# Layer norm's affine on the vector engine, a new order of routing and first expert, and a branch moved, in a two-layer decoder trunk

## The chip, the cores and the metric

The kernel runs on one core of a Trainium2 chip. The core has a matrix engine (TensorE, PE in the profile, with its weight loads PEld), a vector engine (VectorE, DVE), a scalar engine (ScalarE, ACT), a programmable engine (GpSimd, POOL), a queue engine that issues DMAs (SyncE, SP) and 16 DMA engines. Each engine works through its own queue in order. The metric is the device time of one execution in microseconds (us), less is better.

## The reference

Two layers work on 512 tokens of width 1024, in float32. Each layer has a mixer (five kinds of attention on one input projection, each gated, summed and sent through one output projection `w_out`) and a hierarchical mixture of experts. After each of the two comes a layer norm of `alpha * h + sublayer`:

```python
h = layer_norm(ALPHA * h + mixer(h), ln1_g, ln1_b)     # (x - mean) * rsqrt(var + eps) * g + b
glog = h @ w_rg + b_rg                                 # 4 groups: the best one
elog = h @ w_re[group] + b_re[group]                   # 4 experts in it: the best two, softmax weights
y = sum over 16 experts e of weight[:, e] * ((silu(a) * u) @ w_down[e]),  a, u = split(h @ w_up[e])
h = layer_norm(ALPHA * h + y, ln2_g, ln2_b)
```

`w_up[e]` is 1024x512 and `w_down[e]` 256x1024. The output is h after the second layer.

## The kernel before, in words

**Products.** Nearly all products are made of three TensorE matmuls: each operand is split into a high part rounded to fp32r (ScalarE, `hi`, line 97) and the rest (a subtraction on VectorE or, for chosen weights, on GpSimd, `lo`, line 112), and high x high, high x low and low x high are summed in PSUM. Split weights live in five buffers (three `wh`, two `eh`), which `hl_slot` hands out in turn; the raw weights come by DMA through SP into 28 slots of 512 KB (20 `rp`, 4 `rw`, 4 `re`).

**Output projection with routing** (`w_out`, `rows_done`). The 512 tokens are four row tiles of 128. The projection works on tiles 0 and 1 over all of K, and then on tiles 2 and 3; of each pair the last five K pieces are done tile by tile, so that a tile ends while the next is still being multiplied. What follows on a finished tile is a Python generator whose steps a counter (`tick`, one per group of three matmuls, the waits given by `gap`) places among the next tile's matmuls: add the residual (line 1044) and take statistics (1045); four transposes per half, copied out by ScalarE (1111); the 20 router logits; mean and rstd (`norm`, whose power is a GpSimd operation); the layer norm itself; `route` (line 1136 to 1162), a chain of some fifteen operations on 4 to 20 columns that marks the two chosen experts in `M` and sums them in `cb`; and `places`, which ranks the tokens of each expert by two small matmuls (1173) and turns ranks into row numbers (`own`, `sidx`). Two indirect DMAs of GpSimd then scatter the tile's normalised rows to `xd`, sorted by expert (1185).

The layer norm is written as one ScalarE operation `(x - mean) * rstd` over 1024 columns (1064), a multiplication by g and an addition of b, both on GpSimd (1066, 1067). For the last tile it is done in halves, one of them on VectorE.

**Expert 0** doesn't wait for the scatter. A column mask per tile (`slots_one`, 1316: which of 112 slots does this token fill) is multiplied with the normalised rows on TensorE (`own_rows`, 1328: 16 matmuls of 112 columns per tile, 64 in all), which yields expert 0's rows already transposed; `expert_x` splits them. In the kernel before, tile 0's masks and products come before the last tile's rank and the other three after it.

**The expert loop** (`experts`, `expert_step`). For each expert of 112 rows at most: four pieces of `w_up` (`expert_up`, 24 matmuls), `swiglu` (ScalarE tanh, two VectorE operations), two transposes, `expert_down` (12 matmuls), while the rows of the next but one are fetched from `xd` (1332), transposed and split (`next_x`). The weights of expert 1 are split while expert 0 is at work. The rest of the routing (softmax weights, gather indices) is `route_rest`. Experts 14 and 15 are not written back: `keep` multiplies their outputs by the weights of the rows and splits them (ScalarE and VectorE, 101 and 113), and the combination multiplies them on TensorE with transposed masks.

**The branch.** If more than 112 tokens chose one expert, `past_capacity` computes the rest. Each engine's queue reads the largest count into a register and compares (line 1482); with these inputs the body is skipped. Before, this stands behind the `keep` of expert 14's output, whose PSUM bank (`pt`) the body would use.

**Order.** The program is traced in the order of the Python code; a scheduler then puts each engine's instructions in order by a model of the times, earlier code first among those ready, and sets semaphores. `issue_after(i)` forces the instructions of a block that run on i's engine behind i in that engine's queue.

Of the kernel before, what the change touches and what calls it, by code (L numbers as in the profile page):

```python
# [15 lines left out]
ALU = mybir.AluOpType  # L16
AX = mybir.AxisListType

P = 128
# [51 lines left out]
class Trunk:  # L71
# [51 lines left out]
    def tr(self, out, in_, k=P):  # L123
        self.nc.tensor.transpose(out, in_, self.ident[:k, :k])  # L124
# [817 lines left out]
    def affine(self, out, x, gb):  # L942
        self.nc.vector.tensor_tensor(out, x, gb[0], ALU.mult)
        self.nc.gpsimd.tensor_tensor(out, out, gb[1], ALU.add)
# [91 lines left out]
    def rows_done(self, t, o, hr, gb, pool):  # L1036
# [12 lines left out]
        if t == NT - 1:  # L1049
# [13 lines left out]
        for n in ((slice(0, D),) if t < NT - 1 else self.halves):  # L1063
            self.normed = nc.scalar.activation(hr[:, n], hr[:, n], AF.Identity, bias=shift, scale=r)
            e = nc.vector if n.stop == 512 else nc.gpsimd
            e.tensor_tensor(hr[:, n], hr[:, n], gb[0][:, n], ALU.mult)
            e.tensor_tensor(self.h1[:, t, n], hr[:, n], gb[1][:, n], ALU.add)
        mb = self.route(t, lg)
        yield self.gap[2]
        if t == NT - 1:  # L1070
            self.xT = self.sb(self.base, [P, 2, 2, KT, CAP], "xh", F32R)
            self.yb = self.sb(self.base, [P, 4, D], "xl")
            with self.tc.issue_after(added.ins):
                self.own_rows(0, range(self.own0, self.nown))
        self.places(t, mb)
        if t == NT - 1:
# [27 lines left out]
    def logits_in(self, x, half, pool):  # L1104
# [6 lines left out]
        self.nc.scalar.copy(xT, ps.rearrange("p (k q) -> p k q", q=P))  # L1111
# [29 lines left out]
    def route(self, t, lg):  # L1141
# [17 lines left out]
        V.tensor_copy(self.ev[:, t], v[:, 0, 0:2])  # L1159
        mb = self.sb(rp, [P, 16], "mb", BF16)  # L1160
        V.tensor_tensor(mb, M[:, 0], M[:, 1], ALU.add)
        V.tensor_tensor(self.cb[:, t + 1, :], self.cb[:, t, :], mb, ALU.add)
        return mb

    def places(self, t, mb):
# [13 lines left out]
        V.scalar_tensor_tensor(self.own[:, t], mb, -65536.0, slot, ALU.mult, ALU.add)  # L1179
# [3 lines left out]
        self.routed = V.tensor_copy(self.sidx[:, t, :], si)  # L1183
        for c in range(2):
# [61 lines left out]
    def swiglu(self, ps, pool, tag, n=P):  # L1246
# [3 lines left out]
        nc.scalar.activation(t, ps[:n, :DE], AF.Tanh, scale=0.5)  # L1250
# [4 lines left out]
    def past_capacity(self, l):  # L1255

        nc, A = self.nc, self.A
        for t in range(NT):
# [7 lines left out]
            for e in range(NE):  # L1266
# [10 lines left out]
                y = [self.ps("pt"), self.ps("pt")]  # L1277
# [8 lines left out]
    def load_pieces(self, l, n):  # L1286

        nc, A = self.nc, self.A
        while len(self.pieces) < min(n, 6 * NE):
# [4 lines left out]
            if j < 4:  # L1294
                v = t.rearrange("p (k f) -> p k f", k=2)
                nc.sync.dma_start(v, A["w_up"][l, e, 256 * j : 256 * j + 256, :].rearrange("(k p) f -> p k f", p=P))
            else:
                v = t.rearrange("p (k f) -> p k f", k=1)
                nc.sync.dma_start(v, A["w_down"][l, e, P * (j - 4) : P * (j - 3), :].rearrange("(k p) f -> p k f", p=P))
# [6 lines left out]
    def expert_split(self, n):  # L1306

        if n not in self.hl:
            tag, pool = self.hl_slot()
            self.hl[n] = self.split_w(self.pieces[n], tag, "pool" if (n % 6 in self.pool_lo if n >= self.npre else n in self.pre_pool) else "dve", pool)  # L1310
# [7 lines left out]
    def own_rows(self, e, ts):  # L1318
# [3 lines left out]
        for t in ts:  # L1322
            one = self.one[:, t]
            self.slots_one(one, e, t)
# [12 lines left out]
    def expert_x(self, e):  # L1337

        xh, xl = self.xT[:, e % 2, 0], self.xT[:, e % 2, 1]
        for g in range(2):  # L1340
# [9 lines left out]
            self.lo(xl[:, 4 * g : 4 * g + 4, :], v, xh[:, 4 * g : 4 * g + 4, :])  # L1350

    def expert_up(self, l, e, j):
# [5 lines left out]
        h, lw = self.expert_split(6 * e + j)  # L1358
# [6 lines left out]

# [319 lines left out]
```

## Time and profile before

| what | before |
|---|---|
| time, median of 3 runs | 1724.15 us (1722.12 to 1728.31) |
| the profiled execution | 1725.9 us, its span 1723.8 us |
| mean granted clock of TensorE | 0.967 |
| busy: TensorE, VectorE, ScalarE, GpSimd | 1608.3, 1257.8, 893.2, 356.6 us |
| DMA | 273.60 MB, mean 159 GB/s |

In a profile each row of a timeline is an instruction or a run of like ones: start, duration, engine, line, tile written and tiles read, count, and in brackets how long the engine had nothing to do before it and what ended that. [...] A wait that an engine's queue makes without a data operation shows as the queue (DVEq, PEq). Layer 0's projection with routing runs from about 585 to 665 us, its expert loop to 830; layer 1's from about 1436 to 1515 and to 1681. Output of layer 1's combination ends the span.

### The profile page before, as it was taken

The page shows a single profiled execution, that of the slowest core. Times are in us where ns is not written, and L with a number is a line of the kernel's source. Part 1 is how long each engine was busy: PE and PEld are TensorE (multiplying, and loading weights), DVE is VectorE, ACT ScalarE, POOL GpSimd, SP SyncE. Part 2 cuts the span into 40 slices and gives each one's busy share as a digit, 9 for nine tenths or more (in the row PEclk, how much of TensorE's full clock was granted, in tenths as well). Part 3 has the DMA queues.
Part 4 walks back from the last instruction along what each step waited for, and adds up shares of the span by engine and source line. Part 5 has one row for each costly group of instructions (what it writes and reads, how often), then busy time and mean ns, then how long its engine had stood idle before and what let it go on. Part 6 is the DMA issues. An engine that isn't in the chain of part 4 may idle for free. (4 is left out here: it accounts for less than half of the span.)

```text
span 1723.8 us, 22844 instructions
## 1 busy us (share of the span) xinstructions
PE 1608.3 (93%) x7936; PEld 1272.9 (74%) x7936; DVE 1257.8 (73%) x2512; ACT 893.2 (52%) x1689; POOL 356.6 (21%) x261
## 2 busy tenths in 40 slices
PE   8999999999999988999699999999999999789994
PEld 7877877787778766666587787777877787666672
DVE  6776648755794679988688756588567757798876
ACT  5644446443463434888456434464344634368872
POOL 0000011111112254333510000110101123533345
PEclk9999999989999988999799999999999999899997
DMA  8232322444329547997542222222322285499953
GB/s 252 62 95 71 78 67 62 118 103 124 105 78 316 192 161 236 385 379 278 187 141 62 83 86 66 77 61 85 101 79 62 86 301 180 152 313 381 377 182 125
DMA packets 254561, 273.60 MB, mean 159 GB/s; under 512 B 38666, under 2 KB 191360, under 8 KB 254432
## 3 DMA queue, kind: packets, MB, share of 16 engines
q1 hardware_dynamic: 241032, 223.98, 40.6%
q0 software_dynamic: 13312, 47.98, 8.0%
q8 instruction: 67, 1.10, 0.3%
q14 instruction: 62, 0.51, 0.1%
q10 hardware_dynamic: 88, 0.03, 0.0%
HBM read 239.18 MB, written 32.77 MB: 158 GB/s over the span
## 5 line engine op out<-in xcount | busy, mean ns | idle before, releaser
L161 PE MATMUL f<-xh,wh 128*128 128x512 f32 (+2 forms) x1920 | 631.2, 397 | 2.1 <-DVE ot L587 1.1
L161 PEld LDWEIGHTS f<-xh,wh 128*128 128x128 f32 (+1 forms) x1920 | 355.6, 188 | 76.9 <-ACT xh L97 1.3
L161 PE MATMUL f<-xl,wh 128*128 128x512 f32 (+2 forms) x960 | 381.0, 397 | 0.0
L793 POOL TENSOR_TENSOR mg<-mg,gt 128x512 f32<-128x512 f32 x64 | 96.7, 1511 | 978.4 <-DVE gt L792 978.4
L112 DVE TENSOR_TENSOR wh<-rw,wh 128x1024 fp32r<-128x1024 f32 (+3 forms) x172 | 228.1, 1332 | 52.1 <-ACT wh L97 50.8
L161 PEld LDWEIGHTS f<-xl,wh 128*128 128x128 f32 (+1 forms) x960 | 180.8, 188 | 36.7 <-DVE xl L112 0.2
L97 ACT CAST wh<-rw 128x1024 fp32r<-128x1024 f32 (+3 forms) x178 | 178.6, 1012 | 47.2 <-PE f L187 13.9
L783 ACT ACTIVATE gt<-f,bgh 128x512 f32<-128x512 f32 x80 | 55.1, 688 | 209.6 <-PE f L161 209.6
L116 PE MATMUL f<-wh,xh 128*112 128x512 f32 (+1 forms) x564 | 154.7, 402 | 3.1 <-DVE wh L112 2.1
L116 PE MATMUL f<-oh,bh 128*128 128x512 f32 x480 | 131.2, 400 | 0.1
L116 PEld LDWEIGHTS f<-wh,xh 128*112 128x112 f32 (+1 forms) x564 | 98.3, 179 | 33.8 <-DVE wh L112 3.3
L97 ACT CAST pth<-pt 128x128 fp32r<-128x128 f32 (+1 forms) x192 | 77.5, 418 | 87.2 <-PE pt L124 81.4
L792 DVE SCALAR_TENSOR_TENSOR gt<-gt,f 128x512 f32<-128x512 f32 x64 | 43.8, 685 | 105.6 <-PE f L116 101.1
L116 PE MATMUL f<-eh,xh 128*112 128x512 f32 (+1 forms) x396 | 112.0, 409 | 9.0 <-DVE eh L112 9.0
L112 DVE TENSOR_TENSOR ptl<-pt,pth 128x128 fp32r<-128x128 f32 (+1 forms) x192 | 88.9, 474 | 24.7 <-ACT pth L97 20.6
L97 ACT CAST wh<-rp 128x1024 fp32r<-128x1024 f32 x84 | 87.4, 1054 | 34.0 <-PE pt L116 20.7
L116 PE MATMUL s<-qk,qk 128*128 128x256 f32 (+7 forms) x416 | 98.3, 334 | 5.7 <-DVE st L249 2.6
L116 PEld LDWEIGHTS f<-oh,bh 128*128 128x128 f32 x480 | 88.9, 190 | 19.8 <-issue 1.0
L112 DVE TENSOR_TENSOR wh<-rp,wh 128x1024 fp32r<-128x1024 f32 x70 | 95.0, 1366 | 10.9 <-ACT wh L97 10.0
L116 PEld LDWEIGHTS f<-eh,xh 128*112 128x112 f32 (+1 forms) x396 | 69.9, 182 | 29.8 <-DVE eh L112 10.3
L124 PE MATMUL pt<-ident,ne 128*128 128x128 f32 x472 | 83.7, 279 | 8.5 <-DVE ne L428 3.8
L116 PEld LDWEIGHTS s<-qk,qk 128*128 128x128 f32 (+1 forms) x416 | 66.9, 192 | 26.5 <-DVE st L249 9.3
(366 smaller groups left out, 2851.4 us busy)
## 6 DMA issues: line engine op xcount, KB each, us to landing
rp<-in_w_up_dram SPq DMA_DIRECT2D x96, 512.0 KB, 14.1
rw<-in_w_gate_dram SPq DMA_DIRECT2D x80, 512.0 KB, 3.8
rp<-in_w_down_dram SPq DMA_DIRECT2D x48, 512.0 KB, 13.1
rw<-in_w_in_dram SPq DMA_DIRECT2D x38, 512.0 KB, 3.7
rw<-in_w_out_dram SPq DMA_DIRECT2D x32, 512.0 KB, 4.2
yd<-xl POOLq DMA_DIRECT2D x28, 448.0 KB, 7.0
xl<-xd POOLq DMA_DIRECT2D x24, 448.0 KB
rb<-in_w_br_dram SPq DMA_DIRECT2D x80, 128.0 KB, 3.0
```

Source lines behind the costliest of these rows:

```text
L97: return nc.scalar.copy(out, in_)
L112: return e.tensor_tensor(out, in_, hi.bitcast(F32), ALU.subtract)
L116: self.nc.tensor.matmul(out, lhsT, rhs, start=start, stop=stop)
L124: self.nc.tensor.transpose(out, in_, self.ident[:k, :k])
L161: self.nc.tensor.matmul(o[:M, n], a[:, k, :M], b[:, k, n], start=c + k + m == 0, stop=k == KT - 1 and m == 2, skip_group_check=cut > 1)
L783: nc.scalar.activation(t, gp, AF.Tanh, bias=self.bgh[:, b * 8 + f : b * 8 + f + 1], scale=0.5)
L792: nc.vector.scalar_tensor_tensor(t, t, 1.0, bp, ALU.add, ALU.mult)
L793: i = nc.gpsimd.tensor_tensor(m, m, t, ALU.add)
```

## The change

1. *Affine.* `mean_rstd` replaces `norm` in `rows_done` and leaves out the product of mean and rstd. The layer norm of the mixer is two VectorE operations per half row: `(x - mean) * g`, then `* rstd + b`; ScalarE and GpSimd no longer take part. They stand behind `counted`, the running count at the end of `route`. Tile 2's second half, and its scatter, come only after tile 3's `counted`; tile 3's halves come in `places`, behind its `own` and the mask for expert 0 and ahead of the row numbers `sidx`.
2. *Routing and selection.* The copy of the two maxima (`ev`) moves behind the count. `places` of a tile comes 4 ticks after its route (before 12). The masks for tiles 0 and 1 are made in tile 2's step and their products stand behind tile 3's logits; tiles 2 and 3 follow tile 3's rank.
3. *First splits.* No split of the projection's weights is on GpSimd. The four high parts of expert 0's `w_up` come behind the last copy of the transposed rows, their low parts, all on VectorE, behind the split of expert 0's rows. `first_up` orders expert 0's 24 matmuls by kind: eight high x high, eight low rows x high weights, eight high rows x low weights.
4. *Other orders in expert 0.* Weight loads from piece 28 on are held in SP's queue behind the load of the rows of expert 3. Expert 1's first splits come behind expert 0's tanh (high) and gate (low), its transposes behind expert 0's. One low part on GpSimd comes behind the last scatter.
5. *Branch.* The branch stands ahead of the `keep` of expert 14; its body takes the `s` banks in place of `pt`.

```diff
-    def split_w(self, raw, tag="wh", eng="dve", pool=None):
+    def after(self, i):
+        return self.tc.issue_after(i.ins) if i else ExitStack()
+
+    def split_w(self, raw, tag="wh", eng="dve", pool=None, after=(None, None)):
...
-        self.hi(h, raw)
-        self.lo(l, raw, h, eng=eng)
+        with self.after(after[0]):
+            self.hi(h, raw)
+        with self.after(after[1]):
+            self.lo(l, raw, h, eng=eng)
...
-        if t == NT - 1:
+        last = t == NT - 1
+        if t == NT - 2:
...
-            with self.tc.issue_after(added.ins):
-                self.own_rows(0, range(self.own0))
+            for i in range(t):
+                self.slots_one(self.one[:, i], 0, i)
         for half in range(2):
             self.logits(lp, xT[half], half)
-        nmu, r, shift = self.norm(st)
+        if last:
+            self.own_rows(0, range(t - 1))
+        nmu, r = self.mean_rstd(st)
...
-        for n in ((slice(0, D),) if t < NT - 1 else self.halves):
-            self.normed = nc.scalar.activation(hr[:, n], hr[:, n], AF.Identity, bias=shift, scale=r)
-            e = nc.vector if n.stop == 512 else nc.gpsimd
-            e.tensor_tensor(hr[:, n], hr[:, n], gb[0][:, n], ALU.mult)
-            e.tensor_tensor(self.h1[:, t, n], hr[:, n], gb[1][:, n], ALU.add)
+        def affine(half):
+            c = slice(512 * half, 512 * half + 512)
+            nc.vector.scalar_tensor_tensor(hr[:, c], hr[:, c], nmu, gb[0][:, c], ALU.add, ALU.mult)
+            return nc.vector.scalar_tensor_tensor(self.h1[:, t, c], hr[:, c], r, gb[1][:, c], ALU.mult, ALU.add)
         mb = self.route(t, lg)
+        with self.tc.issue_after(self.counted.ins):
+            if last:
+                self.late()
+            else:
+                affine(0)
+                if t < NT - 2:
+                    affine(1)
+                self.late = lambda: (affine(1), self.scatter(t))
         yield self.gap[2]
...
-        self.places(t, mb)
-        if t == NT - 1:
+        self.places(t, mb, (lambda: self.slots_one(self.one[:, t], 0, t), lambda: affine(0), lambda: affine(1)) if last else ())
+        if t == NT - 2:
+            with self.tc.issue_after(self.routed.ins):
+                self.slots_one(self.one[:, t], 0, t)
+        if last:
             with self.tc.issue_after(self.rank.ins):
-                self.own_rows(0, range(self.nown, NT))
-            self.expert_x(0)
+                self.own_rows(0, [t - 1, t])
+            with self.tc.issue_after(self.routed.ins):
+                self.expert_x(0)
...
+        with self.tc.issue_after(owned.ins):
+            for f in between:
+                f()
...
-                y = [self.ps("pt"), self.ps("pt")]
+                y = [self.ps("s"), self.ps("s")]
...
+            with self.after(self.held):
+                if j < 4:
+                    nc.sync.dma_start(v, A["w_up"][l, e, 256 * j : 256 * j + 256, :].rearrange("(k p) f -> p k f", p=P))
...
+    def first_up(self, l):
+
+        up = self.up[0] = self.ps("f")
+        xh, xl = self.xT[:, 0, 0], self.xT[:, 0, 1]
+        w = [self.expert_split(j) for j in range(4)]
+        for x, i in ((xh, 0), (xl, 0), (xh, 1)):
+            for k in range(KT):
+                self.mm(up[:CAP], x[:, k, :], w[k // 2][i][:, k % 2, :], x is xh and i == 0 and k == 0, i == 1 and k == KT - 1)
...
-        h, lw = self.expert_split(6 * e + 4 + j)
+        h, lw = self.expert_split(6 * e + 4 + j, (None, self.xlo if e + j == 0 else self.scat[-1] if e == 0 else None))
...
-                self.next_x(1)
+                with self.tc.issue_after(turned.ins):
+                    self.next_x(1)
...
-                with self.tc.issue_after((self.routed, self.glu, self.hid[1])[self.upa[j]].ins):
-                    self.expert_up(l, 1, j)
+                self.expert_up(l, 1, j, (self.tanh, self.glu))
...
-        first = self.keep(y, 0, ((self.ap, "pth"), (self.ap, "ptl")))
...
         with self.tc.If(n > self.cap):
             self.past_capacity(l)
+        first = self.keep(y, 0, ((self.ap, "pth"), (self.ap, "ptl")))
...
-                with tc.issue_after(self.routed.ins), tc.issue_after(self.scat[-1].ins):
-                    for j in range(self.npre):
-                        with ExitStack() as st:
-                            if j >= self.nearly:
-                                st.enter_context(tc.issue_after(self.normed.ins))
-                            self.expert_split(j)
+                self.held = i
+                for j in range(self.npre):
+                    self.expert_split(j, (self.copied, self.xlo))
...
-    pre_pool = 3, 4
+    pre_pool = 4,
-    gap, order = (3, 1, 12), "0m1mm021v3v2vc3v"
+    gap, order = (3, 1, 4), "0m1mm021v3v2vc3v"
-    wo_pool = ((1, 1), (1, 3), (1, 5))
+    wo_pool = ()
```

## Rows read from the trace of the kernel before

**Rows 1.** The page's busy time, share of the span and instructions of each engine.

```profile
PE 1608.3 (93%) x7936; PEld 1272.9 (74%) x7936; DVE 1257.8 (73%) x2512; ACT 893.2 (52%) x1689; POOL 356.6 (21%) x261
```

**Rows 2.** Stretch table for PE: stretch, its length, busy us (count), PEclk granted, DMA share, GB/s.

```profile
608.60:622.30 13.70, 12.96 (x43) 0.51 0.49 183
...
622.30:643.40 21.10, 20.88 (x107) 1.00 0.50 183
...
647.00:663.20 16.20, 12.23 (x56) 0.50 0.38 133
...
1476.60:1482.70 6.10, 6.09 (x16) 0.51 0.95 333
```

**Rows 3.** PE's timeline: start us, us, engine, line, operation, [idle before <-releaser].

```profile
607.94 0.50 PE L116 MATMUL f<-eh,xh 128*128 128x512 f32 x1 [2.80 <-DVE eh L112]
...
642.99 0.40 PE L116 MATMUL pv<-wh,xl 128*128 128x512 f32 x1
...
657.37 0.17 PE L1173 MATMUL pt<-mb,trib 128*128 128x16 bf16 x1 [3.97 <-DVE mb L1161]
...
657.39 8.45 PE L1328 MATMUL f<-hr,mg 128*128 128x112 f32 x48
...
673.67 0.96 PE L124 MATMUL s<-ident,xl 112*128 112x112 f32 x8 [1.62 <-DMA xl<-xd]
...
1476.61 0.79 PE L116 MATMUL f<-eh,xh 128*128 128x512 f32 x1 [3.40 <-DVE eh L112]
```

**Rows 4.** DVE's timeline around the routing of layer 0.

```profile
602.70 1.74 DVE L1137 SCALAR_TENSOR_TENSOR gk<-lg,gm,vec 128x4 f32<-128x4 f32 x1
...
645.78 0.68 DVE L1044 SCALAR_TENSOR_TENSOR hr<-hr,pv 128x512 f32<-128x512 f32 x1
...
652.34 0.22 DVE L1137 SCALAR_TENSOR_TENSOR gk<-lg,gm,vec 128x4 f32<-128x4 f32 x1
...
653.14 0.73 DVE L1066 TENSOR_TENSOR hr<-hr,lnp 128x512 f32<-128x512 f32 x1
...
653.91 2.16 DVE L1067 TENSOR_TENSOR mg<-hr,lnp 128x512 f32<-128x512 f32 x1
...
657.14 0.17 DVE L1161 TENSOR_TENSOR mb<-M 128x16 bf16<-128x16 f32 x1
...
658.77 2.35 DVE L112 TENSOR_TENSOR wh<-rp,wh 128x1024 fp32r<-128x1024 f32 x2
```

**Rows 5.** POOL's timeline around the routing of layer 0.

```profile
602.02 2.40 POOL L1067 TENSOR_TENSOR mg<-hr,lnp 128x1024 f32<-128x1024 f32 x1
...
661.13 1.96 POOL L1185 DMA_INDIRECT xd<-mg,sidx  x1 [0.30 <-DVE wh L112]
...
663.12 2.37 POOL L112 TENSOR_TENSOR eh<-rp,eh 128x1024 fp32r<-128x1024 f32 x1
```

**Rows 6.** Timelines of DVE (layer 0) and PE (layer 1) at the expert loop's end.

```profile
828.97 1.41 DVE L113 SCALAR_TENSOR_TENSOR ptl<-pt,rw,pth 112x512 fp32r<-112x512 f32 x2 [2.25 <-ACT pth L101]
...
835.28 0.75 DVE L1496 SCALAR_TENSOR_TENSOR mg<-xl,wc,mg 128x512 f32<-128x512 f32 x1 [4.90 <-DVEq L1482]
...
1684.77 0.76 PE L116 MATMUL f<-ptl,oo 112*128 112x512 f32 x1 [3.79 <-PEq L1482]
```

**Rows 7.** Stretch table, all engines: projection with routing, expert loop, both of layer 0.

```profile
600.00:640.00 40.00, 36.24 (x157) 28.77 (x157) 30.79 (x70) 12.55 (x14) 25.65 (x14) 0.83 0.48 173
...
676.00:804.00 128.00, 119.09 (x576) 87.41 (x575) 114.01 (x135) 104.31 (x148) 42.41 (x35) 1.00 1.04 375
```

**Rows 8.** SP's timeline (DMA issues) around the routing of layer 0.

```profile
661.15 1.64 SPq L1296 DMA_DIRECT2D rp<-in_w_up_dram  x2
...
670.05 1.29 SPq L1332 DMA_DIRECT2D xl<-xd  x3
```

**Rows 9.** Line 1482, the branch, on DVE's queue: durations in ns, first and last start.

```profile
L1482 DVEq COMPARE_BRANCH  x2: 68/70/72, 830.2 to 1680.2; - x2
...
L1482 DVEq EVENT_SEMAPHORE  x2: 21/21/21, 834.9 to 1685.2; - x2
```

More of the change, by code (lines that the diff above doesn't have):

```diff
@@ L940, in norm, with mean_rstd @@
         return mv[:, 0:1], mv[:, 2:3], mv[:, 3:4]
-    def affine(self, out, x, gb):
-        self.nc.vector.tensor_tensor(out, x, gb[0], ALU.mult)
-        self.nc.gpsimd.tensor_tensor(out, out, gb[1], ALU.add)
+    def mean_rstd(self, st):
+        nc = self.nc
+        mv = self.sb(self.rp, [P, 4], "mv")
+        nc.vector.bn_aggr(mv[:, 0:2], st)
+        nc.vector.tensor_scalar(mv[:, 1:2], mv[:, 1:2], LN_EPS, None, ALU.add)
+        nc.gpsimd.tensor_tensor(mv[:, 2:3], mv[:, 1:2], self.mhalf[:, 0:1], ALU.pow)
+        nc.vector.tensor_scalar(mv[:, 3:4], mv[:, 0:1], -1.0, None, ALU.mult)
+        return mv[:, 3:4], mv[:, 2:3]
     def ln_params(self, which, l, pool, tag):
@@ L1110, in logits_in @@
             self.tr(ps[:, j * P : (j + 1) * P], x[:, k * P : (k + 1) * P])
-        self.nc.scalar.copy(xT, ps.rearrange("p (k q) -> p k q", q=P))
+        self.copied = self.nc.scalar.copy(xT, ps.rearrange("p (k q) -> p k q", q=P))
         return xT
@@ L1158, in route, with places @@
             V.tensor_scalar(M[:, c], z[:, 1], v[:, 1, c : c + 1], None, ALU.is_equal)
-        V.tensor_copy(self.ev[:, t], v[:, 0, 0:2])
         mb = self.sb(rp, [P, 16], "mb", BF16)
         V.tensor_tensor(mb, M[:, 0], M[:, 1], ALU.add)
-        V.tensor_tensor(self.cb[:, t + 1, :], self.cb[:, t, :], mb, ALU.add)
+        self.counted = V.tensor_tensor(self.cb[:, t + 1, :], self.cb[:, t, :], mb, ALU.add)
+        with self.tc.issue_after(self.counted.ins):
+            V.tensor_copy(self.ev[:, t], v[:, 0, 0:2])
         return mb
-    def places(self, t, mb):
+    def places(self, t, mb, between=()):
         nc, rp = self.nc, self.rp
@@ L1178, in places @@
         V.tensor_tensor(slot, slot, rank, ALU.add)
[L1179 removed]
+        owned = V.scalar_tensor_tensor(self.own[:, t], mb, -65536.0, slot, ALU.mult, ALU.add)
+        with self.tc.issue_after(owned.ins):
+            for f in between:
+                f()
         si = self.sb(rp, [P, 2], "si")
@@ L1183, in places, with scatter @@
         self.routed = V.tensor_copy(self.sidx[:, t, :], si)
+        if t != NT - 2:
+            self.scatter(t)
+    def scatter(self, t):
+        nc = self.nc
         for c in range(2):
@@ L1349, in expert_x, with expert_up @@
             self.hi(xh[:, 4 * g : 4 * g + 4, :], v)
-            self.lo(xl[:, 4 * g : 4 * g + 4, :], v, xh[:, 4 * g : 4 * g + 4, :])
-    def expert_up(self, l, e, j):
+            self.xlo = self.lo(xl[:, 4 * g : 4 * g + 4, :], v, xh[:, 4 * g : 4 * g + 4, :])
+    def expert_up(self, l, e, j, after=(None, None)):
         if j == 0:
@@ L1357, in expert_up @@
         self.load_pieces(l, 6 * e + j + 1)
-        h, lw = self.expert_split(6 * e + j)
+        h, lw = self.expert_split(6 * e + j, after)
         up = self.up[e][:CAP]
@@ L1379, in experts @@
         self.up = {}
-        for j in range(4):
-            self.expert_up(l, 0, j)
+        self.first_up(l)
         for e in range(NE - 1):
@@ L1566, in layer @@
             pre = self.bufs(pre)
-            self.nhi, self.slot, self.pieces = 0, 0, []
+            self.nhi, self.slot, self.pieces, self.held = 0, 0, [], None
             nrp, nre = self.BUFS["rp"], self.BUFS["re"]
@@ L1612 @@
     orders = ('aaaqaaaaqaaaaaaaaaaaaqqa', 'gggqqgaaaaggaaaaaaggaaaaqqggggggaqqqqagagaaa', 'qaagaaggagqqaggaaaqaggaqaaaaqggaqqaaaaggqggqqggqq', 'ggqgaaaaaaaaaaagqgaaaggqagggggggqqqqgaaaaga', 'ggaaaaaaaaaggggggggaaaaaaaaaaaaaaaagaaaaaaaaaagggagg')
-    nearly = 3
-    upa = 0, 1
-    own0, nown, x1 = 0, 1, 0
-    halves = slice(512, D), slice(0, 512)
+    x1 = 0
     class _Pool:
```

24 lines of the change are left out of this document (9 added, 15 removed).

## The prediction

> **What bounds the kernel now.** I read the busy table first [rows 1]: TensorE is busy for 93% of the span and VectorE for 73%, so the kernel is TensorE's except where TensorE stands still or runs slowly. The slices of the page show such places at the same points of both layers: the output projection with the routing, and the end of the expert loop. Next came the stretch table with the granted clock [rows 2]. [...] Then TensorE's timeline [rows 3]: 2.80 us of idle time at 607.94 until VectorE had a weight half ready (it has a twin of the same size in layer 1, and a third stall there of 3.40 us); 3.97 us at 657.37 until the last tile's routing had its mask; 1.62 us at 673.67 until expert 1's rows had arrived. The low clock begins each time after TensorE sat idle or nearly so.
>
> Why VectorE is late is told by its own rows beside GpSimd's [rows 4, 5]. L1137 works on four numbers per partition. It takes 0.22 us at 652.34 and 1.74 us at 602.70, where it ends at 604.44; GpSimd's half of the affine, begun at 602.02, ends at 604.42. L1067 on VectorE (2.16 us from 653.91 against 0.73 for L1066, same shape) shows the same: VectorE stands still until a GpSimd operation on SBUF data is done. I count thirteen such places between 600 and 672 us, 1 to 2.4 us each, about 20 us; all but one lie under operations that this change takes from GpSimd.
>
> **The change, part by part.** The sum is made on the profiled execution: 1725.9 us, 2.1 more than its span, 1.75 more than the median of the runs (1724.15).
>
> *Projection (A).* Removed per layer: from GpSimd two operations of 2.40 us for each of three tiles, two halves for the fourth, and four weight splits of about 2.4 us (such a one is the row at 663.12); from ScalarE the normalisation. Added on VectorE: four fused operations per tile. The nearest row is L1496 with two SBUF operands and the same shape, 0.75 us [rows 6], so 3.0 us per tile, 12 per layer; and the four splits (three here, one after) at 1.2 us each (two in 2.35 us at 658.77), 4.8. It loses the 2.9 us of the last tile's half and about 18 us of standing still. VectorE's own balance is thus some 4 us in favour, and it has 9 us idle in 600 to 640 to fill [rows 7]. What TensorE can win: 2.80 idle plus half of the 12.96 busy us at clock 0.51, 9.2 us in layer 0; 2.8 + 3.4 + half of 6.09 in layer 1, 9.2 as well. I don't take all: VectorE now carries three more splits and two tiles' affine in the same stretch, which leaves it some 90% full, and a split queued behind 3 us of affine makes TensorE wait again. Bounds: 9.2, and 1 where VectorE becomes the limit. I take 6 per layer, nearer to the upper end because short waits (1 us) leave the clock alone in the expert stage, which shows 1.00 throughout [rows 7]. A = 12.
>
> *Routing of the last tile and selection (B).* Before, the last projection matmul ends at 643.4 and the last rank product starts at 657.37, 14.0 us later. VectorE's first addition for the tile came only at 645.78, behind the routing of tile 2. From 652.34 to 657.14 the route takes 4.8 us, of which 653.14 to 656.07 is the affine (2.9). After: the addition at about 645.0 (tile 2's routing ends sooner, but half an affine is queued ahead), 0.7 for it, 0.7 for four transposes, 0.6 for their copy, 1.0 for eight logit matmuls at the full clock, 3.3 for a route without affine and without standing still: 651.3, so 6.1 us sooner. The selection products of tiles 0 and 1 (32 of 64 matmuls) fit into that wait, where 16 went before; that also keeps TensorE from idling. After the rank, 32 matmuls are left and not 48 in 8.45 us. But they wait for VectorE, on which there now stand, one behind the other, tile 2's second affine half (1.5), four place operations and one selection column (0.8), and tile 3's affine (3.0): 5.3 us after the rank, then eight matmuls of 0.18, so 6.7. The four low halves of the first weights now all come behind the split of the rows (1.5 us later), 4.8 us on VectorE, while the new order gives TensorE 16 matmuls that need none of them. The last matmul of the first product then ends some 13.1 us after the rank; 14.7 before. One GpSimd split falls on these VectorE operations: 0 to 2.4 us as in [rows 5], I take 1.2. The rest of the routing (about 4 us on VectorE, before under the selection products) now falls into the expert loop, where VectorE is busy 114.01 of 128 us [rows 7]: free to 4 us, I take 1.5. Together 6.1 + 0.4 - 1.5 = 5 per layer; bounds 9 (nothing given back) and 0. B = 10.
>
> [...]
>
> *Scatter and loads.* Tile 2's scatter moves behind route 3 and half an affine, and tile 3's indices come after 3 us of affine, so the scatters end about 9.5 us after the rank; before 5.7 (661.13 + 1.96) [rows 5]. The load of expert 1's rows was issued at 670.05, 7 us after that, with weight loads issued ahead of it on SP [rows 8]. Those are now held behind it; with the memory to itself I take 3.5 us for the scatter to land and 3 for the load: 16 after the rank, as before (16.3). TensorE reaches those rows after the first expert's transposes, 15 to 16 after the rank. So I cost this at 0, bounds -1.6 (the wait at 673.67 goes) and +4. Holding back four weight loads costs nothing while the loop draws on 28 pieces ahead.
>
> *Smaller edits.* The copy of the two maxima behind the count and one operation less in the mean: 0.2 each, in the terms above. Places after 4 ticks instead of 12: in A. Expert 1's splits behind the gate's operations: 0, bounds -1 and +1; one VectorE operation of 1.2 sets both.
>
> *Branch (C).* VectorE weights expert 14's output until 830.4, then branches; its next operation starts at 835.28 after 4.90 us [rows 6]. Its compare starts at 830.2 and 1680.2, the event behind it at 834.9 and 1685.2 [rows 9], 4.7 and 5.0 us. With the branch ahead, it begins when the last split is done, some 3 to 4 us sooner, and the weighting (1.41) comes behind. So VectorE gains 2 to 3 us at each layer's end. TensorE's 3.79 us at 1684.77 shrinks by less, as its own branch comes no sooner than its last matmul. I take 2 in layer 0, where ScalarE's branch is next, and 3 in layer 1, whose tail is one chain. Bounds 0 and 4 each. C = 5.
>
> Sum: 12 + 10 + 5 = 27; 1725.9 - 27 = 1698.9, 1697 against the median. I say 1698.
>
> **Rivals.**
> 1. *VectorE becomes the bound of the projection.* For it: some 90% full by the count above, one queue in a fixed order. Against: the stalls of 2 us each go. A falls to 2 per layer, B to 3: 4 + 6 + 5 = 15, so 1711 (this and the next times on the profiled execution).
> 2. *The branch gives nothing.* TensorE's own branch ends when it did, and the weighting only moves behind: C = 0, 1704. [...]
> 3. *The loop is paced by its loads.* DMA share 1.04 through the expert stage [rows 7]. Then B is lost and four held loads of 1.4 us (0.52 MB at 375 GB/s) cost 5.6 in each layer: 27 - 10 - 11 = 6, 1720. Against: no TensorE wait there is on a weight load.
> 4. *Slower: expert 1's rows come late.* The scatter goes behind 3 us of affine and another scatter, and TensorE's order puts the transposes ahead of matmuls that could run. If the rank comes no sooner (it must gain under 4 us for this to decide), the wait grows by 4 us, the clock drops, and some 10 busy us at half speed cost 5: 9 per layer, with A and B at nothing: +18 - 5, 1739.
>
> **How the numbers follow.** My forecast 0.58 (own range 1689 to 1706), rival 1 0.20, rival 2 0.08, rival 3 0.06, rival 4 0.08. The low end takes A and B at their upper bounds (-18 - 18) and C at 5: 1685, against the median 1683. The high end passes rival 1 and stops short of rival 3: 1717. A change under 0.3%, 5.2 us, can't be told from none. Rival 3 lies at that bound, most of it within; with the upper edge of rival 1 that makes 0.06 for the same, 0.08 for slower (rival 4), 0.86 for faster.
>
> **What would show it.** Right: no VectorE operation of 16 columns over 1 us before the rank product; TensorE's clock at 1.00 from 600 to 640 us; from the last projection matmul to the last rank under 10 us; 32 selection matmuls behind it; VectorE's wait for the branch ended before 832. Wrong: TensorE waits over 2 us for a weight half in the projection, or for expert 1's rows; splits stretched to 2.4 us with GpSimd idle; a branch that ends where it did.

## The result, and the profile after

The changed kernel takes 1698.31 us (median of 4 runs, 1694.69 to 1704.04) against 1725.2 before: ratio 0.9847, 95% interval 0.981 to 0.9885. In a second comparison it is 0.9846 (0.9826 to 0.9866). The profiled execution takes 1701.36 us, its span 1699.6, 24.2 less than before. The forecast was 1698; how it was reached held less well than the number.

The span can be cut at instructions that both kernels have, so that each stage has a length of its own. These rows are from TensorE's timeline of the kernel before; the other cuts stand in [rows 3]:

```profile
577.68 0.50 PE L116 MATMUL f<-wh,xh 128*128 128x512 f32 x1
...
758.65 0.38 PE L124 MATMUL pv<-ident,sw 112*128 112x112 f32 x2
...
822.62 0.35 PE L124 MATMUL pv<-ident,sw 112*128 112x112 f32 x2
...
838.91 0.64 PE L124 MATMUL pv<-ident,gt 112*128 112x112 f32 x2 [1.79 <-DVE mg L1496]
...
1427.86 0.73 PE L116 MATMUL f<-wh,xh 128*128 128x512 f32 x2
...
1494.20 0.40 PE L116 MATMUL pv<-wh,xl 128*128 128x512 f32 x1
...
1507.34 0.17 PE L1173 MATMUL pt<-mb,trib 128*128 128x16 bf16 x1 [3.68 <-DVE mb L1161]
...
1608.95 0.38 PE L124 MATMUL pv<-ident,sw 112*128 112x112 f32 x2
```

The same view of the changed kernel: first and last projection matmul, last rank product, the selection products behind it, three transposes that waited for a late gate in the expert loop, the transposes of the ninth expert (e = 8), those on both sides of the branch, and layer 1:

```profile
577.49 0.73 PE L116 MATMUL f<-wh,xh 128*128 128x512 f32 x2
...
632.51 0.40 PE L116 MATMUL pv<-wh,xl 128*128 128x512 f32 x1
...
641.65 0.17 PE L1198 MATMUL pt<-mb,trib 128*128 128x16 bf16 x1 [2.77 <-DVE mb L1184]
...
643.37 5.77 PE L1361 MATMUL f<-hr,mg 128*128 128x112 f32 x24 [0.57 <-DVE mg L1081]
...
672.78 0.41 PE L124 MATMUL pv<-ident,sw 112*128 112x112 f32 x2 [1.31 <-DVE sw L1286]
683.84 0.61 PE L124 MATMUL pv<-ident,sw 112*128 112x112 f32 x2 [2.05 <-DVE sw L1286]
696.40 0.39 PE L124 MATMUL pv<-ident,sw 112*128 112x112 f32 x2 [1.63 <-DVE rw L1272]
...
746.44 0.38 PE L124 MATMUL pv<-ident,sw 112*128 112x112 f32 x2
...
810.40 0.35 PE L124 MATMUL pv<-ident,sw 112*128 112x112 f32 x2
...
820.87 1.96 PE L124 MATMUL s<-ident,rw 128*128 128x128 f32 x8 [3.09 <-ACTq L1522]
824.53 0.61 PE L124 MATMUL pv<-ident,gt 112*128 112x112 f32 x2 [1.70 <-DVE gt L1286]
...
1413.92 0.95 PE L116 MATMUL f<-wh,xh 128*128 128x512 f32 x3
...
1469.00 0.40 PE L116 MATMUL pv<-wh,xl 128*128 128x512 f32 x1
...
1478.15 0.17 PE L1198 MATMUL pt<-mb,trib 128*128 128x16 bf16 x1 [2.78 <-DVE mb L1184]
...
1585.54 0.38 PE L124 MATMUL pv<-ident,sw 112*128 112x112 f32 x2
```

The differences of these starts (us), with those of the fifteenth and sixteenth experts' transposes, which bracket the branch:

| stage | layer 0, before to after | layer 1 | won in both |
|---|---|---|---|
| first to last projection matmul | 65.3 to 55.0 | 66.3 to 55.1 | 21.6 |
| to the last rank | 14.4 to 9.1 | 13.1 to 9.2 | 9.2 |
| to the ninth expert's transposes | 101.3 to 104.8 | 101.6 to 107.4 | -9.3 |
| to the fifteenth's | 64.0 to 64.0 | 64.0 to 64.0 | 0 |
| over the branch to the sixteenth's | 16.3 to 14.1 | 16.4 to 14.7 | 3.9 |
| all else (start, attention, tail) | | | -1.2 |

The sum is 24.2. Of the last row, -0.9 lies behind layer 1's branch, from the sixteenth expert's transposes to the end of the span (34.5 to 35.4 us). The projection won nearly twice what was forecast; what the routing won, the first experts gave back in full.

The stretch table (length, then busy us of PE, PEld, DVE, ACT, POOL; granted clock as a share of full speed; DMA share; GB/s) of the changed kernel shows both:

```profile
600.00:640.00 40.00, 38.88 (x225) 32.38 (x225) 34.92 (x118) 15.77 (x19) 7.83 (x7) 1.00 0.51 175
660.00:700.00 40.00, 35.02 (x166) 26.27 (x165) 38.04 (x67) 29.23 (x42) 11.68 (x10) 0.96 1.04 382
```

Against [rows 7], GpSimd's 25.65 us in 600 to 640 have become 7.83 and the clock 0.83 has become 1.00. VectorE does 34.92 of 40, and up to the last projection matmul (600 to 632.5) TensorE waits for none of it: it is busy for 32.50 of 32.50 us. In 660 to 700 VectorE is full (38.04 of 40). There POOL's and DVE's timelines show why two of the gates are late:

```profile
680.32 2.47 POOL L112 TENSOR_TENSOR wh<-rp,wh 128x1024 fp32r<-128x1024 f32 x1 [1.14 <-ACT wh L97]
...
692.71 2.43 POOL L112 TENSOR_TENSOR wh<-rw,wh 128x1024 fp32r<-128x1024 f32 x1 [1.22 <-issue]
```

```profile
680.47 2.35 DVE L1248 TENSOR_TENSOR rw<-rw 128x8 f32<-128x8 f32 x1
...
682.81 0.41 DVE L1285 SCALAR_TENSOR_TENSOR sw<-sw,f 112x256 f32<-112x256 f32 x1
...
692.88 2.28 DVE L1267 TENSOR_TENSOR rw<-rw 128x8 f32<-128x8 f32 x1
695.09 0.41 DVE L1285 SCALAR_TENSOR_TENSOR sw<-sw,f 112x256 f32<-112x256 f32 x1
```

L1248 and L1267 belong to `route_rest` and work on eight numbers per partition, for which the other operations of `route_rest` take 0.15 to 0.17 us in this stretch. They last until GpSimd's split ends (682.79, 695.14), and the gate (L1285) stands behind them: those are TensorE's waits of 2.05 and 1.63 us. Before, `route_rest` lay at 662 to 671 us, under the selection and expert 0's first product; two of its operations lasted 2.59 and 2.38 us there too, and no gate had to wait for them.

### The profile page after: what moved, and what is told of

Same layout as the page of the kernel before. It is cut to its first block, busy times and chain, and to the rows that moved or that the text cites. A ratio compares the mean times of both kernels' runs of the same rounds, so it can differ in the third digit from the quotient of the medians.

```text
span 1699.6 us, 22822 instructions
## 1 busy us (share of the span) xinstructions
PE 1596.7 (94%) x7936; PEld 1265.4 (74%) x7936; DVE 1244.5 (73%) x2540; ACT 882.9 (52%) x1679; POOL 299.8 (18%) x237
## 5 line engine op out<-in xcount | busy, mean ns | idle before, releaser
L112 DVE TENSOR_TENSOR wh<-rw,wh 128x1024 fp32r<-128x1024 f32 (+1 forms) x174 | 228.0, 1316 | 51.8 <-ACT wh L97 50.7
L97 ACT CAST wh<-rw 128x1024 fp32r<-128x1024 f32 (+3 forms) x178 | 178.5, 1012 | 49.6 <-PE f L192 14.1
L797 DVE SCALAR_TENSOR_TENSOR gt<-gt,f 128x512 f32<-128x512 f32 x64 | 43.7, 684 | 105.8 <-PE f L116 101.3
L124 PEld LDWEIGHTS pt<-ident,ne 128*128 128x128 f32 x472 | 54.8, 141 | 42.4 <-issue 17.1
## 6 DMA issues: line engine op xcount, KB each, us to landing
rp<-in_w_down_dram SPq DMA_DIRECT2D x48, 512.0 KB, 13.1
```

Source lines behind the costliest of these rows:

```text
L97: return nc.scalar.copy(out, in_)
L112: return e.tensor_tensor(out, in_, hi.bitcast(F32), ALU.subtract)
L124: return self.nc.tensor.transpose(out, in_, self.ident[:k, :k])
L797: nc.vector.scalar_tensor_tensor(t, t, 1.0, bp, ALU.add, ALU.mult)
```

## The experiments

All in one table, by the cuts above (layer 0 / layer 1). The last column is fifteenth to sixteenth expert, over the branch. The medians of the kernel before in the three comparisons were 1728.88 (affine_back, branch_back, rest_hid, rest_spread), 1727.7 (before_affine2, the two pool kernels, first_old) and 1726.76 us (the other four).

| kernel | time us (runs) | projection | to rank | to ninth expert | branch |
|---|---|---|---|---|---|
| changed, again (after_again) | 1702.06 (5) | 55.1 / 55.1 | 9.2 / 9.2 | 104.9 / 106.7 | 13.9 / 15.3 |
| affine_back | 1715.97 (4) | 63.2 / 61.4 | 11.3 / 11.2 | 104.3 / 104.9 | 14.0 / 14.6 |
| split_back | 1711.68 (1) | 63.9 / 60.7 | 7.9 / 7.9 | 106.3 / 106.3 | 13.9 / 13.4 |
| before_affine2 | 1716.25 (5) | 60.9 / 62.4 | 10.6 / 10.6 | 103.6 / 103.9 | 16.0 / 16.9 |
| pool_read | 1721.65 (1) | 56.0 / 56.0 | 9.9 / 9.9 | 115.4 / 115.0 | 14.0 / 13.9 |
| pool_write | 1701.07 (1) | 55.1 / 55.1 | 9.2 / 9.3 | 106.1 / 106.9 | 13.4 / 14.2 |
| branch_back | 1702.31 (4) | 55.0 / 55.0 | 9.1 / 9.1 | 103.3 / 107.4 | 15.5 / 17.0 |
| first_old | 1698.76 (1) | 55.1 / 55.1 | 9.2 / 9.2 | 103.8 / 103.8 | 14.2 / 15.2 |
| rest_hid | 1693.36 (4) | 55.1 / 55.1 | 9.2 / 9.2 | 105.9 / 105.6 | 13.8 / 13.9 |
| rest_spread | 1695.74 (4) | 55.1 / 55.0 | 9.1 / 9.1 | 104.1 / 105.4 | 13.9 / 14.8 |
| rest_fine | 1691.81 (5) | 55.1 / 55.0 | 9.2 / 9.2 | 103.4 / 102.3 | 13.8 / 13.8 |
| rest_fine_old | 1692.93 (5) | 55.1 / 55.1 | 9.2 / 9.2 | 103.3 / 102.1 | 13.9 / 14.7 |

The projection's length repeats within 0.1 us where nothing in it is changed; the loop's does not. The changed kernel's order gives 103.3 to 104.9 us in layer 0 (three profiles, branch_back among them) and 106.7 to 107.4 in layer 1.

**What made the projection faster.** Three kernels undo or do one part.

affine_back:

```diff
-        nmu, r = self.mean_rstd(st)
+        nmu, r, shift = self.norm(st)
...
-            nc.vector.scalar_tensor_tensor(hr[:, c], hr[:, c], nmu, gb[0][:, c], ALU.add, ALU.mult)
-            return nc.vector.scalar_tensor_tensor(self.h1[:, t, c], hr[:, c], r, gb[1][:, c], ALU.mult, ALU.add)
+            nc.scalar.activation(hr[:, c], hr[:, c], AF.Identity, bias=shift, scale=r)
+            nc.gpsimd.tensor_tensor(hr[:, c], hr[:, c], gb[0][:, c], ALU.mult)
+            return nc.gpsimd.tensor_tensor(self.h1[:, t, c], hr[:, c], gb[1][:, c], ALU.add)
```

> The changed kernel with the layer norm's affine put back on ScalarE (normalise) and GpSimd (two operations per half); the new order of routing, splits, selection and loads stays. Theory (the standing-still of VectorE under GpSimd operations is what cost the time in the projection): the projection slows to half clock again, last projection matmul some 8 to 11 us later in each layer, and the last rank later too; time about 1718 to 1726. Rival (the reordered first splits and routing made the gain): within 4 us of the changed kernel, 1695 to 1703, and TensorE's clock stays 1.00 from 600 to 640.

split_back:

```diff
-    wo_pool = ()
+    wo_pool = ((1, 1), (1, 3), (1, 5))
```

> The changed kernel with the three low halves of the projection's weights split on GpSimd again. Theory (GpSimd's splits hold VectorE as its affine did): the last projection matmul 4 to 8 us later per layer and TensorE at half clock for part of 600 to 640. Rival (with the affine gone GpSimd's splits find VectorE with room): within 1.5 us.

before_affine2, on the kernel before (the affine of all four tiles, both halves, behind the count):

```diff
-        for n in ((slice(0, D),) if t < NT - 1 else self.halves):
-            self.normed = nc.scalar.activation(hr[:, n], hr[:, n], AF.Identity, bias=shift, scale=r)
-            e = nc.vector if n.stop == 512 else nc.gpsimd
-            e.tensor_tensor(hr[:, n], hr[:, n], gb[0][:, n], ALU.mult)
-            e.tensor_tensor(self.h1[:, t, n], hr[:, n], gb[1][:, n], ALU.add)
...
+        for half in range(2):
+            c = slice(512 * half, 512 * half + 512)
+            with self.tc.issue_after(self.counted.ins):
+                self.normed = nc.vector.scalar_tensor_tensor(hr[:, c], hr[:, c], nmu, gb[0][:, c], ALU.add, ALU.mult)
+                nc.vector.scalar_tensor_tensor(self.h1[:, t, c], hr[:, c], r, gb[1][:, c], ALU.mult, ALU.add)
```

> The kernel before with one edit: the layer norm's affine as fused VectorE operations behind the count of each tile, nothing on ScalarE and GpSimd for it; the three first weight splits stay on GpSimd and the routing, selection and loads keep their order. Theory (the affine on GpSimd, under which VectorE stands still, is the bulk of the projection's gain): the last projection matmul comes 7 to 10 us earlier in layer 0, about as much in layer 1; time 1706 to 1712. Rival (affine and split moves only work together, since the three splits left on GpSimd still hold VectorE): under 4 us per layer, 1718 or more.

The stretch tables of PE for the changed kernel (its first stretch stands above), affine_back, before_affine2 and split_back, in this order:

```profile
1435.00:1475.00 40.00, 40.00 (x236) 1.00 0.50 174
```

```profile
600.00:640.00 40.00, 35.76 (x175) 0.91 0.51 173
1435.00:1475.00 40.00, 36.02 (x181) 1.00 0.55 193
```

```profile
600.00:640.00 40.00, 36.34 (x180) 0.91 0.50 174
1435.00:1475.00 40.00, 37.20 (x171) 0.87 0.49 174
```

```profile
600.00:640.00 40.00, 36.02 (x165) 0.87 0.50 173
1435.00:1475.00 40.00, 36.02 (x179) 0.96 0.51 193
```

Rows of POOL, DVE and PE in split_back, with the affine on VectorE:

```profile
602.98 2.50 POOL L112 TENSOR_TENSOR eh<-rw,eh 128x1024 fp32r<-128x1024 f32 x1 [5.99 <-ACT eh L97]
```

```profile
603.12 2.39 DVE L1173 TENSOR_TENSOR el<-lg,goh 128x16 f32<-128x16 f32 x1
```

```profile
609.99 0.17 PE L1198 MATMUL pt<-mb,trib 128*128 128x16 bf16 x1 [3.98 <-DVE mb L1184]
```

An operation on 16 columns lasts until GpSimd's split ends (605.48), another (L1178) 2.07 us under the next split, and TensorE waits 3.98 us for the mask at the end of this chain.

With either the affine or the three splits on GpSimd, TensorE waits again (2.03 us at 619.33 in affine_back, 2.81 at 608.33 in before_affine2, 3.98 in split_back), and in three of the four stretches of the undone halves the clock falls (0.91, 0.87 and 0.96). Putting the affine back costs 8.2 and 6.4 us, the splits 8.8 and 5.6; the affine alone on the old kernel wins 4.4 and 3.9 of 10.3 and 11.3. The parts don't add: the whole gain needs GpSimd free of both. The mechanism holds in all three, at the lower edge of its price or a little under in affine_back, and at half of it in before_affine2, whose rival (the moves only work together; under 4 us without the splits) came nearer than the theory (7 to 10).

**What holds VectorE.** pool_read and pool_write add work on GpSimd alone (`powed` is the reciprocal root on GpSimd; in pool_write the loop body is `nc.gpsimd.memset(idle, 0.0)`):

```diff
+        with self.tc.issue_after(self.powed.ins):
+            idle = self.sb(pool, [P, 128], "idle")
+            for i in range(16):
+                nc.gpsimd.tensor_tensor(idle, gb[0][:, :128], gb[1][:, :128], ALU.mult)
```

> The changed kernel with work added on GpSimd alone: per row tile, behind the reciprocal root, 16 multiplications of 128 columns that read two operands of SBUF, with a result nobody reads. Theory (VectorE operations with two SBUF operands stand still while GpSimd works on SBUF operands of this kind): several such VectorE operations per tile take 1 to 2.5 us in place of 0.2 to 0.75, the clock falls to half in 600 to 640 again and the last rank comes 5 to 10 us later per layer. Rival (the old affine cost by its place in the chain of dependences): GpSimd is busy some 5 us more per tile and nothing else moves; last rank within 1 us.

> The changed kernel with the same 16 added GpSimd operations per tile as writes of a constant, which read no operand. If VectorE stands still for any GpSimd work, as pool_read; if it takes GpSimd operations that read two SBUF operands, VectorE's operations keep 0.2 to 0.75 us and the last rank stays within 1 us of the changed kernel's.

The direction was right and the place wrong. The projection is 1.0 us longer with reads and the clock in 600 to 640 stays 1.00; the last rank is 1.7 us late, not 5 to 10. Pool_read's POOL, DVE and PE timelines:

```profile
639.75 15.33 POOL L1077 TENSOR_TENSOR idle<-lnp 128x128 f32<-128x128 f32 x24
655.34 1.05 POOL L1223 DMA_INDIRECT xd<-mg,sidx  x1 [0.25 <-issue]
```

```profile
636.77 1.05 DVE L1084 SCALAR_TENSOR_TENSOR hr<-hr,mv,lnp 128x512 f32<-128x512 f32 x1
...
655.12 0.29 DVE L1245 TENSOR_TENSOR rbig<-M,own 128x128 f32<-128x128 f32 x1 [3.57 <-POOL idle L1077]
```

```profile
668.78 1.54 PE L124 MATMUL s<-ident,xl 112*128 112x112 f32 x7 [5.05 <-DMA xl<-xd]
```

The fused operation takes 1.05 us in place of 0.74, so VectorE is held by GpSimd operations that read, but by short ones (0.46 us each in the median) only briefly. Most of pool_read's 20 us lies elsewhere. To the ninth expert it loses 10.6 and 7.6 us against the changed kernel. Of these, 4.1 and 2.1 come ahead of expert 0's transposes, where VectorE above all stands idle for 3.57 us until the last added operation is done (655.12): a dependence that the edit brought with it, beside the work. The other 6.5 and 5.5 come behind them, with scatters that stand behind the added work: the first starts at 655.34, 12 us after the rank (2 in the changed kernel), and TensorE waits 5.05 us for expert 1's rows.

Pool_write leaves the projection and the rank in place; VectorE's fused operations take 0.74 to 0.75 us beside its writes. So in this pair the added reads hold VectorE (1.05 us for the fused operation) and lengthen the projection by 1.0 us, and the added writes do neither. It isn't a pair of equal length, though: a write takes 0.20 us in the median, less than half of a read.

**The branch.** branch_back moves one line back (and the body's PSUM banks):

```diff
+        first = self.keep(y, 0, ((self.ap, "pth"), (self.ap, "ptl")))
...
         with self.tc.If(n > self.cap):
             self.past_capacity(l)
-        first = self.keep(y, 0, ((self.ap, "pth"), (self.ap, "ptl")))
```

> The changed kernel with expert 14's weighting put ahead of the branch again. Theory (in the changed kernel the branch starts to be resolved while TensorE still works on expert 14, which gives 2 us per layer): 1702, 4 us slower than the changed kernel. Rival (the branch hides nothing, its time is in the chain in both orders): within 1 us of the changed kernel.

By its total the rival is right: its ratio 0.9844 (0.9814 to 0.9874) equals the changed kernel's. By its stage the theory is: 15.5 and 17.0 us over the branch, where eleven profiles with the branch ahead have 13.4 to 14.2 and 13.4 to 15.3 (means 13.9 and 14.4), and the three with it behind have 15.5 to 16.3 and 16.4 to 17.0 (means 15.9 and 16.8). That is 2.0 and 2.4 us, less than what totals of single kernels differ by. In layer 1 about 1 us of it is lost again behind the cut: from the fifteenth expert's transposes to the end of the span the same profiles take 49.4 us with the branch ahead and 50.9 with it behind (means). TensorE's row in branch_back, and VectorE's after the branch in the changed kernel:

```profile
821.92 1.94 PE L124 MATMUL s<-ident,rw 128*128 128x128 f32 x8 [5.70 <-DVEq L1523]
```

```profile
L1522 DVEq COMPARE_BRANCH  x2: 68/70/72, 813.9 to 1652.8; - x2
...
L1522 DVEq EVENT_SEMAPHORE  x2: 21/21/21, 820.6 to 1659.0; - x2
```

From compare to event it now takes 6.7 and 6.2 us on VectorE (4.7 and 5.0 in [rows 9]), but it begins under TensorE's work (the compare at 813.9 us, TensorE's matmuls until 817.8).

**What the expert loop gave back.** rest_hid, rest_spread and rest_fine move `route_rest`; here is rest_hid's edit and the form of the other two, in which `yield` cuts the function into four parts (with experts 4 to 7) or eleven (with experts 3 to 13), each behind the hidden split of the expert ahead:

```diff
-                with self.tc.issue_after(self.routed.ins):
+                with self.tc.issue_after(self.hid[1].ins):
                     self.route_rest()
```

```diff
-                with self.tc.issue_after(self.routed.ins):
-                    self.route_rest()
+                rest = self.route_rest()
+            if self.rest <= e < self.rest + 11:
+                with self.tc.issue_after(self.hid[1].ins):
+                    next(rest)
```

> The changed kernel with the rest of the routing (weights of the gates, gather indices) issued behind expert 2's hidden split and so later in the loop, after its tight start. Theory (the 5 us per layer that experts 1 to 3 give back come from two of its small VectorE operations that stand still for 2.3 us under GpSimd's weight split ahead of the gate): 2 to 4 us per layer come back, 1691 to 1695. Rival (its 4 us of VectorE work are the cost wherever they lie in the loop, or the give-back is the loop's own pace): within 1.5 us of the changed kernel.

> The changed kernel with the rest of the routing in four parts, each issued behind the hidden split of one of experts 3 to 6, where GpSimd is idle in the changed kernel's trace. If VectorE has about 1 us free per expert there, the whole give-back of the rest, 4 to 5 us per layer, is won: 1688 to 1692, and faster than rest_hid. If the loop is paced by VectorE, the work costs its 4 us wherever it lies: 1697 to 1700. If the give-back comes from the first experts' loads and splits, experts 1 to 3 still lose 5 us and the time stays at 1698.

> The changed kernel with the rest of the routing in eleven parts of one to three VectorE operations, each behind the hidden split of one of experts 3 to 13, and none of them just ahead of an expert's gate. Theory (a small VectorE operation that stands ahead of a gate is held 2 us by GpSimd's weight split; it is that, not the 4 us of work, that delays the loop): no 1.7 us waits of TensorE for the gate as in rest_spread, the ninth expert's transposes 102 to 103 us behind the last rank in place of 104 to 107, time 3 to 4 us per layer below the changed kernel. Rival (VectorE's work itself is the pace): no better than rest_spread, 104 to 105 us.

rest_hid and rest_spread come to 104.1 to 105.9 us: the work costs wherever it lies, it seems. (Rest_hid's time fell into its forecast, but not by the gain that it was forecast from: its two loops together are no faster.) But rest_spread's POOL, DVE and PE rows show the same picture as before, three experts later:

```profile
709.61 2.77 POOL L112 TENSOR_TENSOR eh<-rp,eh 128x1024 fp32r<-128x1024 f32 x1 [1.16 <-ACT eh L97]
```

```profile
710.04 2.37 DVE L1251 TENSOR_SCALAR rw<-rw 128x8 f32<-128x8 f32 x1
712.33 0.41 DVE L1289 SCALAR_TENSOR_TENSOR sw<-sw,f 112x256 f32<-112x256 f32 x1
```

```profile
713.34 0.38 PE L124 MATMUL pv<-ident,sw 112*128 112x112 f32 x2 [1.74 <-DVE sw L1290]
```

At the next two experts L1265 (2.15 us at 721.24) and L1276 (2.36 at 732.22) stand in the same way, each with the gate behind it, and TensorE waits 1.76 and 1.73 us. In rest_fine no such operation stands there, and TensorE's waits in that stretch are those of any expert (0.65 to 0.73 us from 703 to 760):

```profile
704.70 2.57 PE L116 MATMUL pt<-wh,hT 128*112 128x512 f32 x10 [0.67 <-DVE hT L113]
```

The same work now costs next to nothing (fifth to ninth expert 41.1 and 41.4 us; 41.1 before, 43.4 in rest_spread). So the rival that prices VectorE's work itself falls; what costs is the place ahead of a gate under GpSimd's split.

The whole loop ends 1.5 and 4.4 us sooner than in the changed kernel of the same comparison, and 2.1 and 0.7 us of the give-back are left. Not all of this can be put down to the edit, since part of a loop's length is TensorE's clock. From rank to ninth expert TensorE idled 7.5 and 7.9 us before, 10.7 and 12.0 in the changed kernel and 9.6 and 9.7 in rest_fine; the granted clock was 0.97 in both layers before, 0.95 and 0.94 in the changed kernel, 0.95 and 0.97 in rest_fine. Branch_back has the changed order and idles 10.7 us in layer 0, but at 0.97, and takes 103.3 us, no more than rest_fine. So the 1.5 us of layer 0 lie within what the clock alone moves; the 4.4 of layer 1 are more than that. There the changed order took 106.7 to 107.4 us at 0.94 in all three profiles, and 2.1 of the 4.4 us are idle time.

The largest wait that rest_fine has left is one of the same kind, at expert 0's transposes:

```profile
652.16 3.38 DVE L112 TENSOR_TENSOR wh<-rp,wh 128x1024 fp32r<-128x1024 f32 x1
```

```profile
656.38 0.41 PE L124 MATMUL pv<-ident,sw 112*128 112x112 f32 x2 [3.36 <-DVE sw L1297]
```

VectorE's weight split of 1.22 us begins just behind GpSimd's (652.09 to 654.46), lasts 3.38 us, and expert 0's gate stands behind it. In the changed kernel this costs TensorE 3.44 us in layer 1; in layer 0 GpSimd's split was the one to be held (3.46 us), VectorE's took 1.22, and TensorE waited 1.45.

rest_fine has the shortest time here: ratio 0.9796 (0.9782 to 0.9809), beside 0.9846 (0.9826 to 0.9866) for the changed kernel in the same comparison. Only 5.9 of the 12.6 us between the two profiled spans lie in the loops and 1.6 over the branches; 2.8 lie ahead of layer 0's projection, where TensorE's order is the same in both. Rest_hid's total (0.9792, 0.9771 to 0.9813) can't be told from it, though its loops are slower: its projection starts 4.4 us sooner than the changed kernel's. How much of these totals is chance stays open.

**Expert 0's order.** first_old and rest_fine_old put the up matmuls of expert 0 back:

```diff
-        self.first_up(l)
+        for j in range(4):
+            self.expert_up(l, 0, j)
```

> The changed kernel with expert 0's up matmuls in the old order, weight piece by weight piece (high by high, low, high by low in each), in place of all high products first. Theory (B's end: the new order lets TensorE start before the low halves are there): from the last rank to expert 0's transposes 16.5 to 19 us in place of 15.5, time 1 to 3 us per layer longer. Rival (expert 0's products end by VectorE's splits in either order): within 0.5 us.

> rest_fine with expert 0's up matmuls also in the old order, weight piece by piece. From first_old (103.8 us from the last rank to the ninth expert's transposes, against 104.8 and 107.4 in the changed kernel) the order of expert 0 is worth 0 to 1.5 us per layer by itself; if the two gains add, 101.5 to 102 us and 1689 to 1692 in all, the fastest of all; if both only remove the same wait, as rest_fine within 0.5 us.

In first_old TensorE waits 2.00 us for a low half, and expert 0's transposes come 18.8 us behind the rank (15.5 and 17.5 in the changed kernel), as the theory said; the 1 to 3 us per layer that it put on the time don't show. By the ninth expert it is level in layer 0 and some 3 us ahead in layer 1 (103.8 in both), with `route_rest` where it was. With rest_fine's order both variants come to 102.1 to 103.4. So the new order brings expert 0 forward and the loop takes it back: it is worth nothing, and the gains don't add. Two different edits thus win back some 3 us or more in layer 1: in first_old, too, fewer operations of `route_rest` are held ahead of a gate (one of 1.93 us, in place of the two of 2.3).

> The changed kernel once more, beside the next three on one chip: 1694 to 1704, and from the last rank to the hidden-layer transposes of the ninth expert 104 to 108 us per layer as in its first profile.

It came out as in the first profile (table).

## Why the prediction was right, and which of its terms were not

**A, forecast 12, measured 21.6.** The mechanism held: no wait of TensorE's and clock 1.00 from 600 us to the last projection matmul, GpSimd's operations the cause. Two sizes were off. The upper bound of 9.2 per layer counted only the long waits; those of [rows 3] with two short ones (0.74 and 0.22 us, at 611.76 and 628.96) and half of the 12.96 us at 0.51 make 10.2, nearly the whole gain of layer 0 (10.3). In layer 1 the clock of a stretch of the kernel before was missed:

```profile
1450.00:1476.60 26.60, 19.88 (x93) 0.92 0.40 141
```

It lost 6.7 us of waiting, 6.2 of which the prediction had counted, and about 2 of clock, which it hadn't; with 3.05 for [rows 2]'s last row that is about the 11.3 won. And the discount to 6, for a VectorE that would be 90% full, was wrong: it is 87% full (34.92 of 40) and delays nothing. Rival 1 fell with it.

**B, forecast 10, measured -0.1.** The routing chain gave 5.2 and 4.0 us (6.1 forecast), with 32 selection matmuls behind the rank, no small VectorE operation over 1 us, and 9.1 us from the last projection matmul to the rank. The step that failed is "the rest of the routing ... now falls into the expert loop ...: free to 4 us, I take 1.5": from expert 0's transposes to the ninth expert's it lost 5.1 and 5.8 us (84.2 to 89.3 and 89.9), and from the rank on, where expert 0 had won 1.6 and 0, 3.5 and 5.8. Its place was named and its mechanism wasn't. VectorE's idle time was weighed against 4 us of work, while the price was VectorE operations ahead of a gate that a split of GpSimd's holds up: two of 0.15 us that last 2.3, and weight splits of 1.2 us that last up to 3.4. The 1.2 us set aside for a collision with GpSimd's split covered one such meeting in expert 0; one came in nearly each of the first four experts. TensorE's idle time accounts for 3.1 and 4.1 of the 3.5 and 5.8 us, and the granted clock is lower with it (0.95 and 0.94 against 0.97). rest_fine shows that 4.4 of layer 1 can be had back; in layer 0 no gain beyond the clock's is shown.

**C, forecast 5, measured 3.9 in the profiled pair, 4.4 over all profiles, about 1 less with the tail.** VectorE's compare starts under TensorE's last matmuls (at 813.9 us; they end at 817.8) and its event comes at 820.6, before the 832 of the forecast. Layer 1 won less than 3, and part of that is lost again in the tail, as rival 2 had it; that nothing would be won is out by layer 0. The compare by itself takes 68 to 72 ns on VectorE's queue here, but the queue's next event comes 6.2 to 6.7 us after it, so the compare's own time doesn't price the branch.

**Scatter and rows, forecast 0.** The wait at 673.67 in [rows 3] is gone; rival 4 didn't decide, since the rank came 15.7 us sooner. Pool_read shows its mechanism at work where the scatters do come late. Rival 3 (loads): the changed kernel's only wait of TensorE for a weight between rank and branch is 0.41 us in expert 0 of each layer, for VectorE's half, and rest_fine's loop is faster at about the same DMA share in 676 to 804 us (0.96 against 0.97).

So 9.6 us too little in A and 10.1 too much in B cancelled. That the total was right is luck: the mechanisms of A and C held, but the two large terms were each off by about 10 us.

## What to carry to other kernels

When work left GpSimd here, the gain was all of what VectorE and TensorE had lost under it, short waits and half clock (0.51 in [rows 2]) included; count these from the waits rather than discount them. When work moves into a tight loop, ask in front of what it will stand: here an operation of 0.15 us ahead of a gate, under GpSimd's operation of 2.4 us, cost TensorE a wait of up to 2.05. And cut the span at instructions common to both kernels; totals here couldn't see 4 us that the stages showed.

## What was not expected of the hardware

The same instructions in the same order were granted different clocks. One stretch of layer 0's attention, in the changed kernel and in rest_fine (PE, PEld, DVE, ACT, POOL):

```profile
362.00:380.00 18.00, 17.63 (x70) 14.59 (x70) 7.86 (x25) 5.17 (x18) 1.87 (x2) 0.72 0.50 121
```

```profile
362.00:380.00 18.00, 17.57 (x82) 14.66 (x82) 10.25 (x26) 5.17 (x18) 3.86 (x4) 0.91 0.55 132
```

TensorE is as busy in one as in the other, but at 0.72 it does 70 matmul records and at 0.91 82. By its end rest_fine is 2.7 us ahead. In rest_hid a step of 1.6 us comes on top, near 315 us (granted clock 1.00 in 306 to 326 us, against 0.91), and its projection starts 4.4 us sooner than the changed kernel's, before anything that the edits touch. That is as much as several of the edits are worth.
